# Moving the gate transposes of the second layer from one step to two and a half steps behind their silu

## The chip, the cores and the metric

The kernel runs on one core of one Trainium2 chip. The metric is the device time of one execution in microseconds, as the median of several runs: 821.22 us before (three runs, 821.09 to 822.02). Beside it stands one execution taken by the hardware profiler; all rows shown below are from that one.

## The reference

Two residual layers over 256 tokens of width 2048, in float32. The first is retention plus latent attention, gated by SiLU. The second, around which the change lies, is a Conformer convolution module:

```python
def layer_conformer_conv(x, norm_g, w_in, conv_w, conv_b, ln_g, ln_b, w_out):
    h = rms_norm(x, norm_g)
    a, b, gate = jnp.split(h @ w_in, 3, axis=-1)
    u = a * jax.nn.sigmoid(b)
    u = lax.conv_general_dilated(u, ...31 taps, causal, depthwise...) + conv_b
    u = jax.nn.silu(layer_norm(u, ln_g, ln_b))
    return x + (u * jax.nn.silu(gate)) @ w_out
```

Each of `a`, `b` and `gate` has 2048 columns, so `w_in` is 2048 x 6144 and `w_out` 2048 x 2048.

## The kernel before

**Products in three matmuls.** A float32 product is made from halves: `whi` is the weight rounded to the fast matmul type and `wlo` the rest; the activations are split in the same way. `mm3` (lines 193 to 195) issues three matmuls: high by high, high by low and low by high. ScalarE makes `whi` (line 167), VectorE or GpSimd makes `wlo` (`tt`, line 88). SyncE's queue loads the raw weights, 1 MB at a time, into three buffers (line 152).

**Steps and a clock.** The order on TensorE, ScalarE and VectorE is the order in which the program issues its instructions. The program keeps a clock of its own: each half of a weight unit (`half`) advances it to the next whole step, first queueing the `wlo` three steps ahead and the `whi` four steps ahead; `tick(True)` in the middle of a step advances it by a half. `later(n, f)` puts `f` on a list, and the tick at which n steps have gone by runs it, so that its instructions land in the queues at that point. A step of the second layer holds 12 matmuls with 512 columns each.

**A chunk.** `chunk` computes 512 columns for both halves of the tokens into two PSUM tiles of the pool `mm` (four tiles), in eight steps. The second layer runs eight chunks for `a` and `b` (`glu`), four for `gate`, and then the output product: its first half (`u_co1`) into the four tiles of the pool `aux`, sixteen steps, its second half in two more chunks.

**The gates.** After each of the four gate chunks, `gate(c, ps)` lets ScalarE make silu of the two PSUM tiles into two tiles of a pool of six (line 1137), scaled by the norm's factor per token. The result has tokens on the partitions; the output product wants features there. So `turned` issues eight transposes on TensorE (line 1142), which write back into the same PSUM tiles, and `place` lets ScalarE copy these into the gate buffer `cgt` (line 1147) and sets `gates[0]`, the count of gate pairs at hand.

**The convolution and its norm.** While the chunks run, VectorE computes the 31 taps of 16 channel blocks, paced by the clock. When the last sums are made (`sums_end`), `norm_conv` is put 4.5 steps ahead (`LN_LAG`). It issues two pairs of matmuls that sum over the partitions (lines 1013 and 1014), a chain on VectorE and ScalarE (`rs_chain`), and a table load for silu (line 1021). A gate chunk that ends between `sums_end` and `norm_conv` is held: its silu is issued in `norm_conv`, behind that table load. Here this is the third chunk (c = 2), whose silu is issued one and a half steps into the fourth chunk. The fourth gate (c = 3) is issued at the first step of the output product.

**What reads the gates.** From `norm_conv` on, eight pairs of channel blocks go through five stages, half a step apart, a new pair every two steps: normalize on VectorE (`za`), silu on ScalarE (`zs`, line 1035), times the gate on VectorE (`zb`, line 1040), round on ScalarE (`zr`, line 1044), subtract on VectorE (`zc`). `z_run` puts `zb` of pair j off by half a step while `gates[0]` is not above j. Pairs 0 to 3 read the gates of c = 0 and 1; pairs 4 and 5 those of c = 2; pairs 6 and 7 those of c = 3. `zrhs` gives the output product its activations and forces stages that are still open.

Of the kernel before, what the change touches and what calls it, by code (L numbers as in the profile page):

```python
# [48 lines left out]
def body(ctx, tc, a):  # L49
# [22 lines left out]
    def tmp(dt=F32):  # L72
        return tpool.tile([P, 512], dt, tag="t", name=nm("t"))
# [28 lines left out]
    def later(n, fn):  # L102
        due.append((clock[0] + n, len(due), fn))
# [1030 lines left out]
    def gate(c, ps):  # L1134
        g = [tmp(), tmp()]
        for t in range(2):
            act(g[t][:, :], ps[t][:, :], AF.Silu, scale=R1[:, t:t + 1])

        def turned():
            for i in range(4):  # L1140
                for t in range(2):
                    nc.tensor.transpose(ps[i // 2][:, (i % 2) * T + t * P:(i % 2) * T + (t + 1) * P], g[t][:, i * P:(i + 1) * P], ident[:, :])  # L1142

        def place():
            for b in range(2):
                o = (c % 2) * 1024 + b * 512
                act(cgt[c // 2][:, o:o + 512], ps[b][:, :], AF.Copy)
            gates[0] = 2 * c + 2

        later(1, turned)  # L1150
        later(1.5, place)

    for c in range(4):
        ps = chunk(u_cg[4 * c:4 * c + 4], yrhs)

        def gate_when(c=c, ps=ps):
            if held and not ln_done[0]:
                held[0].append(lambda: gate(c, ps))
            else:
                gate(c, ps)  # L1160

        later(0.5, gate_when)
# [135 lines left out]
```

## Time and profile before

| | us |
|---|---|
| median of three runs | 821.22 |
| profiled execution | 824.06 |
| its span, first to last instruction | 822.2 |
| TensorE busy | 811.8 |
| VectorE busy | 595.3 |
| ScalarE busy | 433.6 |
| GpSimd busy | 221.8 |

The profiled execution's time is 1.86 us longer than its span, which runs from the first to the last instruction. Rows of the timeline give the start, the duration, the engine (PE is TensorE, PEld its weight loads, DVE VectorE, ACT ScalarE, POOL GpSimd), the line of the kernel, the operation with its tiles and the number of instructions merged; what stands in brackets is idle time ahead of it, and what ended it. Matmuls are pipelined, and their ends are modelled, so their starts are the safer reading. The four gate sets lie in the trace at 658.7, 681.9, 711.6 and 732.5 us (line 1142); the output product begins at 729.6 us.

### The profile page before, as it was taken

To read this page: it belongs to the slowest core of one execution; us is meant where nothing else is said; L and a number is where in the kernel's file an instruction comes from. 1 tells how busy PE (TensorE), PEld (TensorE's weight loads), DVE (VectorE), ACT (ScalarE), POOL (GpSimd) and SP (SyncE) were. 2 spreads that over 40 slices of the span, in tenths; PEclk is the share of its full clock that TensorE was granted. 3 is DMA by queue.
4 is the path that set the end of the run, shared out by engine and by line. 5 is a ranking of instruction groups with operands and counts; after the bars stand their busy time and mean duration, and the time that the engine had idled before them with its cause. 6 is when DMAs were issued, how large, how long until landed. Compare 5 with 4: busy or idle time off the path is not lost.

```text
span 822.2 us, 12383 instructions
## 1 busy us (share of the span) xinstructions
PE 811.8 (99%) x4766; PEld 721.9 (88%) x4766; DVE 595.3 (72%) x1093; ACT 433.6 (53%) x621; POOL 221.8 (27%) x127
## 2 busy tenths in 40 slices
PE   8999999999999999999999999999999999899998
PEld 8999999999999999998888888888888878788886
DVE  5788565689678755575555439999999989678542
ACT  6765544537445554664545645554545554676331
POOL 0000000000000000000000188899999989200000
PEclk9999999999999999999999999999999999999999
DMA  8875445525444443456554445545554545445650
GB/s 279 294 286 176 161 159 201 198 96 211 156 154 154 155 154 136 172 206 219 191 205 166 192 176 184 204 159 201 205 188 171 196 171 196 154 164 194 246 189 26
DMA packets 24106, 150.93 MB, mean 184 GB/s; under 512 B 2800, under 2 KB 3952, under 8 KB 6896
## 3 DMA queue, kind: packets, MB, share of 16 engines
q1 hardware_dynamic: 23616, 148.03, 50.3%
q0 software_dynamic: 288, 2.10, 0.6%
q8 instruction: 37, 0.61, 0.3%
q14 instruction: 21, 0.17, 0.1%
q10 hardware_dynamic: 144, 0.03, 0.0%
HBM read 148.04 MB, written 2.10 MB: 183 GB/s over the span
## 4 chain that ended last, share of the span: by engine, by line
PE 94%; DVE 3%; ACT 2%; DMA 1%; issue 0%; SPq 0%; DVEq 0%; ACTq 0%
PE mm L195 28%; PE mm L193 28%; PE mm L194 28%; PE aux L195 2%; PE aux L193 2%; PE aux L194 2%; DVE wlo L88 1%; DMA raw<-in_w_first 1%; DVE s L88 0%; PE mm L1142 0%; DVE t L88 0%; ACT whi L167 0%; PE mm L1108 0%; PE aux L853 0%; PE aux L661 0%
## 5 line engine op out<-in xcount | busy, mean ns | idle before, releaser
L167 ACT ACTIVATE whi<-raw 128x1024 fp32r<-128x1024 f32 (+2 forms) x278 | 286.2, 1037 | 277.9 <-PE mm L195 183.2
L88 DVE TENSOR_TENSOR wlo<-raw,whi 128x1024 fp32r<-128x1024 f32 (+2 forms) x194 | 228.2, 1185 | 109.3 <-PE mm L194 52.1
L193 PE MATMUL mm<-whi,s 128*128 128x512 f32 (+1 forms) x760 | 285.8, 376 | 0.0
L195 PE MATMUL mm<-whi,s 128*128 128x512 f32 (+1 forms) x760 | 283.8, 373 | 0.0
L194 PE MATMUL mm<-wlo,s 128*128 128x512 f32 (+1 forms) x760 | 283.6, 373 | 0.0
L88 POOL TENSOR_TENSOR wlo<-raw,whi 128x1024 fp32r<-128x1024 f32 x84 | 201.5, 2412 | 34.7 <-PE mm L194 20.6
L91 DVE SCALAR_TENSOR_TENSOR aux<-s,cb,aux 128x256 f32<-128x256 f32 x480 | 190.0, 485 | 13.7 <-ACT aux L904 13.7
L193 PE MATMUL mm<-s,whi 128*128 128x256 f32 x636 | 183.4, 288 | 1.0 <-ACT whi L167 1.0
L195 PE MATMUL mm<-s,wlo 128*128 128x256 f32 x636 | 180.5, 284 | 1.3 <-DVE wlo L88 1.3
L194 PE MATMUL mm<-s,whi 128*128 128x256 f32 x636 | 179.8, 283 | 0.0
L195 PEld LDWEIGHTS mm<-whi,s 128*128 128x128 f32 x760 | 142.9, 188 | 25.2
L194 PEld LDWEIGHTS mm<-wlo,s 128*128 128x128 f32 x760 | 143.2, 188 | 23.9
L193 PEld LDWEIGHTS mm<-whi,s 128*128 128x128 f32 x760 | 143.3, 189 | 23.8
L195 PEld LDWEIGHTS mm<-s,wlo 128*128 128x128 f32 x636 | 121.7, 191 | 2.2 <-DVE wlo L88 2.2
L193 PEld LDWEIGHTS mm<-s,whi 128*128 128x128 f32 x636 | 121.8, 192 | 2.0 <-ACT whi L167 1.4
L194 PEld LDWEIGHTS mm<-s,whi 128*128 128x128 f32 x636 | 121.9, 192 | 0.6
L711 POOL MEMSET s<- 64x256 f32 x8 | 2.9, 362 | 234.2 <-PE mm L195 162.7
L890 POOL MEMSET s<- 128x30 f32 x16 | 1.1, 121 | 116.8 <-PE mm L194 101.0
L791 POOL DMA_DIRECT2D s<-in_xt x2 | 1.2, 618 | 97.2 <-PE aux L728 96.8
L193 PE MATMUL aux<-whi,s 128*128 128x512 f32 x64 | 25.0, 390 | 0.0
L195 PE MATMUL aux<-whi,s 128*128 128x512 f32 x64 | 24.9, 389 | 0.0
L194 PE MATMUL aux<-wlo,s 128*128 128x512 f32 x64 | 24.9, 389 | 0.0
(186 smaller groups left out, 550.1 us busy)
## 6 DMA issues: line engine op xcount, KB each, us to landing
raw<-in_c_in SPq DMA_DIRECT2D x48, 1024.0 KB, 4.8
raw<-in_w_in SPq DMA_DIRECT2D x36, 1024.0 KB, 4.8
raw<-in_w_out SPq DMA_DIRECT2D x16, 1024.0 KB, 4.8
raw<-in_c_out SPq DMA_DIRECT2D x16, 1024.0 KB, 4.8
raw<-in_w_rv SPq DMA_DIRECT2D x8, 1088.0 KB, 4.9
raw<-in_w_kvb SPq DMA_DIRECT2D x4, 1024.0 KB, 4.8
raw<-in_w_first SPq DMA_DIRECT2D x7, 512.0 KB, 4.9
raw<-in_w_qb SPq DMA_DIRECT2D x3, 1024.0 KB, 4.9
```

Of the source, the lines that this page charges most:

```text
L88: (eng or V).tensor_tensor(out=out, in0=in0, in1=in1, op=op)
L91: V.scalar_tensor_tensor(out=out, in0=in0, scalar=s, in1=in1, op0=op0, op1=op1)
L167: act(hi[:, :], self.raw[u][:, h * n:(h + 1) * n], AF.Copy)
L193: mm(ps, lh, rh, start=start, stop=False, skip_group_check=True)
L194: mm(ps, lh, rl, start=False, stop=False, skip_group_check=True)
L195: mm(ps, ll, rh, start=False, stop=stop, skip_group_check=True)
L711: G.memset(krz(i)[64 * b:64 * b + 64, :], 0.0)
L791: G.dma_start(x1[i][:, :], a["xt"][:, i * 2048:(i + 1) * 2048])
L890: G.memset(upad(c, 0, TAPS - 1), 0.0)
```

## The change

The two delays of `gate` grow. `later` counts from the tick that issued the silu: the transposes go from 1 to 2.5 steps behind it, and the evacuation with the count of gates from 1.5 to 3 steps. Nothing else is edited.

```diff
@@ -1147,8 +1147,8 @@
                 act(cgt[c // 2][:, o:o + 512], ps[b][:, :], AF.Copy)
             gates[0] = 2 * c + 2
 
-        later(1, turned)
-        later(1.5, place)
+        later(2.5, turned)
+        later(3, place)
 
     for c in range(4):
         ps = chunk(u_cg[4 * c:4 * c + 4], yrhs)
```

## The prediction

> **What bounds the kernel now.** I read the page first, then TensorE's waits, then the timeline around each of the four sets of gate transposes, and last the queues of ScalarE and VectorE behind them.
>
> ```profile
> span 822.2 us, 12383 instructions
> PE   811.8 (99%) x4766; PEld 721.9 (88%) x4766; DVE 595.3 (72%) x1093; ACT 433.6 (53%) x621; POOL 221.8 (27%) x127
> PE 94%; DVE 3%; ACT 2%; DMA 1%; issue 0%; SPq 0%; DVEq 0%; ACTq 0%
> PE mm L1142 <- ACT t L1137: 3.1, 5, 1.9
> PE mm L195 <- DVE wlo L88: 1.3, 3, 0.8
> ```
>
> (Span, busy time by engine and the chain of waits by engine are from the page; the last two rows are TensorE's waits: microseconds in all, times, longest.) TensorE holds 94% of the chain, so the time is its instruction stream plus its pauses. The largest pause in its waits is the one that the diff touches: the transposes (line 1142) wait for the silu (line 1137). A listed wait is only the idle part; the loss is read from starts, against a set that does not wait. That is the second set (c = 1), TensorE's rows in the timeline (start, duration):
>
> ```profile
> 655.13 0.39 PE L195 MATMUL mm<-whi,s 128*128 128x512 f32 x1
> 657.85 0.39 PE L195 MATMUL mm<-whi,s 128*128 128x512 f32 x1
> ...
> 681.69 0.39 PE L195 MATMUL mm<-whi,s 128*128 128x512 f32 x1
> 681.92 1.03 PE L1142 MATMUL mm<-ident,t 128*128 128x128 f32 x8
> 682.72 0.48 PE L193 MATMUL mm<-whi,s 128*128 128x512 f32 x1
> ```
>
> The first two rows are the last matmuls of two successive steps: 12 matmuls in 2.72 us, a pitch of 0.227. One step of the program's clock is such a group. From 681.69 to 682.72 are 1.03 us: one pitch and 0.80 for eight transposes. That price stays wherever they stand.
>
> **The change part by part.** It removes and adds no instruction. Four sets of 8 transposes move in TensorE's queue from 1 to 2.5 steps behind their silu, past 18 matmuls (4.08 us), and four pairs of evacuations (line 1147) from 1.5 to 3 steps in ScalarE's. No DMA is issued by either; nothing is moved past one of SyncE's or GpSimd's instructions.
>
> Sets 0, 2 and 3, TensorE, then ScalarE's rows that they wait for:
>
> ```profile
> 658.73 0.33 PE L1142 MATMUL mm<-ident,t 128*128 128x128 f32 x1 [0.48 <-ACT t L1137]
> 660.04 0.48 PE L193 MATMUL mm<-whi,s 128*128 128x512 f32 x1
> 662.65 0.39 PE L195 MATMUL mm<-whi,s 128*128 128x512 f32 x1
> ...
> 709.35 0.39 PE L195 MATMUL mm<-whi,s 128*128 128x512 f32 x1
> 711.63 0.33 PE L1142 MATMUL mm<-ident,t 128*128 128x128 f32 x1 [1.89 <-ACT t L1137]
> 712.21 0.98 PE L1142 MATMUL mm<-ident,t 128*128 128x128 f32 x7 [0.25 <-ACT t L1137]
> 712.95 0.48 PE L193 MATMUL mm<-whi,s 128*128 128x512 f32 x1
> 717.14 0.39 PE L195 MATMUL mm<-whi,s 128*128 128x512 f32 x1
> ...
> 732.13 0.39 PE L195 MATMUL aux<-whi,s 128*128 128x512 f32 x1
> 733.82 0.48 PE L193 MATMUL aux<-whi,s 128*128 128x512 f32 x1
> ```
> ```profile
> 656.69 1.28 ACT L1137 ACT_TABLE_LOAD   x1
> 657.99 1.27 ACT L1137 ACTIVATE t<-mm,R 128x512 f32<-128x512 f32 x2
> ...
> 709.60 1.28 ACT L1021 ACT_TABLE_LOAD   x1
> 710.89 1.27 ACT L1137 ACTIVATE t<-mm,R 128x512 f32<-128x512 f32 x2
> 712.05 1.06 ACT L167 ACTIVATE whi<-raw 128x1024 fp32r<-128x1024 f32 x1
> ...
> 716.52 1.07 ACT L1147 ACTIVATE s<-mm 128x512 f32<-128x512 f32 x2
> ...
> 731.78 1.24 ACT L1137 ACTIVATE t<-mm,R 128x512 f32<-128x512 f32 x2
> ```
>
> (The fourth set's transposes wait too; its 732.13 row is the last matmul ahead of them.)
>
> 1. Set 0: from 657.85 to 660.04 are 2.19; less 1.03, **1.16 us** lost. ScalarE had a table load and two silus to do, to 659.26. In the new place (2.5 steps after the step's start at 655.36) the transposes come up at 662.16: 2.9 us after the silus. The loss goes.
> 2. Set 2: 712.95 less 709.35 is 3.60; less 1.03, **2.57 us**. This silu waits behind the convolution's norm (its factor's chain, a table load), to 712.16. TensorE would pass 709.58 without a pause and have 18 matmuls more, to 713.66: 1.5 us after the silus. It goes.
> 3. Set 3: 733.82 less 732.13 is 1.69; less 1.03, **0.66 us**. Silus end at 733.02; new place 732.36 plus 4.08, 736.44. It goes. Set 1 loses nothing now and nothing then.
> 4. The clock behind set 2. From the first to the twelfth matmul, set 0 took 662.65 less 660.04, 2.61 us; set 2 took 717.14 less 712.95, 4.19. The difference is **1.58 us**, and the stretches (TensorE, weight loads, VectorE, ScalarE, GpSimd busy; then granted clock) name it:
>
> ```profile
> 682.72:701.76 19.04, 19.04 (x87) 15.78 (x86) 17.51 (x37) 9.78 (x12) 16.69 (x8) 1.00 0.54 194
> 709.58:712.95 3.37, 1.23 (x9) 0.88 (x9) 3.23 (x6) 3.34 (x4) 0.00 (x0) 1.00 0.04 15
> 712.95:717.14 4.19, 4.19 (x14) 3.28 (x13) 3.14 (x5) 2.72 (x6) 0.00 (x0) 0.59 0.64 203
> 732.36:733.82 1.46, 1.22 (x10) 0.88 (x9) 1.46 (x3) 1.46 (x3) 0.00 (x0) 1.00 0.81 213
> 733.82:760.00 26.18, 26.18 (x118) 21.67 (x117) 21.36 (x26) 17.21 (x25) 0.00 (x0) 1.00 0.52 189
> ```
>
> The clock was 0.59 right behind the only long pause, and 1.00 behind the sets with short ones or none. I take it that the pause causes it, and count it in full; its bounds are 0 and 1.58.
>
> [...]
>
> 5. Where the stall goes: weights. TensorE now runs 4.15 us further ahead of VectorE, which splits the weights (wlo) behind the same norm chain:
>
> ```profile
> 704.73 1.62 DVE L88 TENSOR_TENSOR wlo<-raw,whi 128x1024 fp32r<-128x1024 f32 x1 [4.50 <-PE mm L194]
> 712.20 1.22 DVE L88 TENSOR_TENSOR wlo<-raw,whi 128x1024 fp32r<-128x1024 f32 x1
> 715.12 1.23 DVE L88 TENSOR_TENSOR wlo<-raw,whi 128x1024 fp32r<-128x1024 f32 x1 [0.32 <-PE mm L194]
> 722.82 0.68 DVE L88 TENSOR_TENSOR s<-s,t 128x512 f32<-128x512 f32 x1
> 726.47 0.69 DVE L88 TENSOR_TENSOR s<-s,s 128x512 f32<-128x512 f32 x1 [0.50 <-ACT s L1035]
> 728.22 0.69 DVE L88 TENSOR_TENSOR s<-s,t 128x512 f32<-128x512 f32 x1
> raw<-in_c_out SPq DMA_DIRECT2D x16, 1024.0 KB, 4.8
> ```
>
> A split is queued three steps ahead of its matmuls. The one at 712.20 ends at 713.42 and serves the step that starts one step after the new transposes: 713.66 and 0.80 and 2.72, 717.2. Margin 3.8 us. From there VectorE needs 5.40 per two steps (722.82 to 728.22), of which 0.50 is a wait on ScalarE, against TensorE's 5.44; lagging, it can lose that wait and catch up. So the margin holds at 3 to 4 us. ScalarE's whi at 712.05 is queued four steps ahead, with a step more of room. A raw tile asked for when the 712.20 split frees its buffer lands 4.8 us later, at 718.2; its first reader, a whi, is queued one step after 717.2, at 719.9, and has four steps to do its work. Cost 0.
>
> 6. The evacuations: ScalarE spends the same time on them; a pair falls 1.5 steps later and behind a weight copy that waits for the very step in which the transposes run, so it adds no wait there. What reads them (line 1040) asks for set 3's part 3.5 steps later, 9.5 us, and for set 2's 6 steps later. The silu tiles are held 4.1 us longer; the next request of that pool after set 2 is set 3's, 6.5 steps on. Behind sets 0 and 1 one tile of squares per pair of channel blocks is asked for, and six buffers hold that beside two silu tiles. PSUM's pair is wanted by another chunk no sooner than five steps after the new evacuation. Cost 0; without this cover, a pair's 1.07 us (716.52) once.
>
> Sum: 1.16 + 2.57 + 0.66 + 1.58 = 5.97. The profiled execution took 824.06 for a span of 822.2; it would take 818.1. The median of the plain runs, 821.22, lies 2.84 below the profiled execution; with the same difference, **815.3 us**.
>
> **The rivals.**
>
> A. The half clock is not in plain runs, or not from the pause. The 2.84 between profiled and plain runs has room for it; against it, no other stretch shows a clock like it. Gain 4.39: 816.8. [...]
>
> B. The wait moves to the weights in part: the split behind the norm is later for TensorE than I count by over 3.8 us. Then the gain of set 2 is mostly lost; sets 0 and 3 stay with 1.82 and perhaps 1 more: about 818.5. Against it: in TensorE's whole wait list, wlo costs 1.3 us.
>
> C. It does not do what it says: the silus of set 2 end after 713.66 too, since the 1.5 us of margin is the smallest. Then only 4.08 of the delay is covered, so hardly anything is left to lose; only if the silus follow TensorE (something later in its queue holds ScalarE) would nothing change: 821.2. The norm chain starts from matmuls that stay in front, which speaks against it.
>
> D. Slower: VectorE sets the pace from the norm to the last layer's product. TensorE gives back the 4.15 us in pieces at wlo, and each piece brings a stretch at 0.59 like the one above, 1.58 each. With four, 5.97 less 4.15 less 6.32 is a loss of 4.5: 825.7; with two, 822.6. It decides from the point where VectorE's two steps cost over 5.44. For it: 5.40 now. Against it: its 0.50 of waiting, and GpSimd's 0.00 in that stretch, so nothing slows VectorE there.
>
> **How the numbers follow.** Forecast 0.64 (815.3; from 814.3, as the plain runs differ by 0.9 among themselves, to 816.2), A 0.22, B 0.07, C 0.04, D 0.03. From 814.3 to 817.8 holds the forecast and A and some of B. A measurement here tells about 0.2%, 1.64 us, from no change: faster means under 819.6. The forecast, A and nearly all of B are faster: 0.92. C and a little of B and D (two stretches) are the same: 0.05; D's rest is slower: 0.03.
>
> **What would show it.** Right: the transposes' wait on the silu gone from TensorE's list; 1.03 us from the matmul ahead of each set to the one behind it; granted clock 1.00 throughout the stretch after the norm; the last matmul some 6 us earlier. Step 4 is wrong if a slow stretch stays without a pause. Step 5 is wrong if waits on wlo or whi appear between the norm and the output product. The prediction is wrong on the whole if TensorE's pauses are gone and the time is not.

## The result and the profile after

The changed kernel took 816.51 us, the median of four executions (816.11 to 816.84), against 821.62 for the kernel before (the three executions known already and a fourth of 823.09). The ratio is 0.9934, 95% interval 0.9921 to 0.9947: faster by 0.7%, or 4.4 to 6.5 us. A second set of executions of both kernels gave 0.9930 (0.9918 to 0.9943). The forecast was 815.3 us, in a range from 814.3 to 817.8.

The page of the changed kernel (span, busy time, chain of waits by engine), and TensorE's waits (microseconds in all, times, longest):

```profile
span 814.3 us, 12383 instructions
PE 808.1 (99%) x4766; PEld 720.7 (89%) x4766; DVE 594.8 (73%) x1093; ACT 434.4 (53%) x621; POOL 221.8 (27%) x127
PE 95%; DVE 2%; DMA 1%; ACT 1%; issue 0%; SPq 0%; DVEq 0%; ACTq 0%
```
```profile
PE aux L243 <- POOL ones L236: 1.0, 1, 1.0
PE mm L193 <- ACT whi L167: 0.8, 1, 0.8
PE mm L195 <- DVE wlo L88: 0.6, 2, 0.3
```

The wait of the transposes on the silu is gone from the list, and nothing has come in its place: the three rows above lie ahead of 640 us, and behind it no wait is listed. The three sets that lost time before, in TensorE's timeline:

```profile
660.02 0.39 PE L195 MATMUL mm<-whi,s 128*128 128x512 f32 x1
660.25 1.03 PE L1142 MATMUL mm<-ident,t 128*128 128x128 f32 x8
661.04 0.48 PE L193 MATMUL mm<-whi,s 128*128 128x512 f32 x1
...
710.35 0.39 PE L195 MATMUL mm<-whi,s 128*128 128x512 f32 x1
710.58 1.03 PE L1142 MATMUL mm<-ident,t 128*128 128x128 f32 x8
711.37 0.48 PE L193 MATMUL mm<-whi,s 128*128 128x512 f32 x1
...
728.94 0.39 PE L195 MATMUL aux<-whi,s 128*128 128x512 f32 x1
729.17 1.03 PE L1142 MATMUL mm<-ident,t 128*128 128x128 f32 x8
729.96 0.48 PE L193 MATMUL aux<-whi,s 128*128 128x512 f32 x1
```

From the matmul ahead of a set to the one behind it are now 1.02 us in all three: eight transposes without a wait. Behind the norm the granted clock is 1.00 throughout (the stretch's columns as in the prediction, the clock third from the end):

```profile
709.58:725.00 15.42, 15.42 (x74) 12.85 (x73) 14.61 (x19) 13.25 (x21) 0.00 (x0) 1.00 0.58 204
```

Two profiled executions differ at their start as well. The chain of waits in order of time shows it; of before, then of after, the last transposes of the second layer's first eight chunks (line 1108) and the last matmul:

```profile
640.10 0.44 PE mm L1108 x4
...
818.19 0.24 PE mm L195
```
```profile
638.19 0.44 PE mm L1108 x4
...
810.25 0.24 PE mm L195
```

At line 1108, ahead of everything that was changed, the profiled execution of before is already 1.91 us late; why stays open. From there to the last matmul it takes 178.09 us and the changed one 172.06: **6.03 us** less. I call this the tail below, and use it for single traces, since the start drops out of it.

### The profile page after: what moved, and what is told of

It reads as the page before. It is cut to its first block, busy times and chain, and to the rows that moved or that the text cites. A ratio compares the mean times of both kernels' runs of the same rounds, so it can differ in the third digit from the quotient of the medians.

```text
span 814.3 us, 12383 instructions
## 1 busy us (share of the span) xinstructions
PE 808.1 (99%) x4766; PEld 720.7 (89%) x4766; DVE 594.8 (73%) x1093; ACT 434.4 (53%) x621; POOL 221.8 (27%) x127
## 4 chain that ended last, share of the span: by engine, by line
PE 95%; DVE 2%; DMA 1%; ACT 1%; issue 0%; SPq 0%; DVEq 0%; ACTq 0%
PE mm L195 28%; PE mm L193 28%; PE mm L194 28%; PE aux L194 2%; PE aux L193 2%; PE aux L195 2%; DMA raw<-in_w_first 1%; DVE wlo L88 1%; DVE s L88 0%; PE mm L1108 0%; PE aux L853 0%; PE mm L1142 0%; PE aux L661 0%; PE aux L759 0%; PE aux L727 0%; PE aux L728 0%
```

## The experiments

**The plain times fall into two groups.** Each execution has a mean granted clock. Beside the kernels below, the kernel before ran 72 times. In 41 of these executions the clock is 0.998 or less, and their median is 822.6 us; in the other 31 it is 0.999 or 1.00, and the median is 820.9. (The groups overlap: the first begins at 821.55, the second ends at 822.28. On the four chips that were used the first group has 11 of 23, 7 of 17, 15 of 21 and 8 of 11.) Of the changed kernel there are ten executions, all at 0.999 or 1.00, with a median of 816.2.

What the mean hides is a stretch at half clock. In the profiled execution of before it is this one (length, TensorE busy, clock, DMA, GB/s):

```profile
713.44:716.84 3.40, 3.40 (x9) 0.50 0.70 214
```

In it matmuls start 0.425 us apart (five from 713.98 to 715.68) instead of 0.227. It costs 3.40 x (1 - 0.227 / 0.425) = 1.58 us when all of it lies on matmuls, and takes 1.70 / 820, or 0.2%, off the mean: so I take 0.998 as the mark of an execution with one such fall. The mean doesn't say where the fall lies, and 3 of the 57 executions of the eight kernels below without a pause over 0.78 us behind the norm are at 0.998 too. That the falls of the kernel before lie behind the third set, in somewhat over half of its executions, is read from the trace and from experiments 3 and 7, not from each execution.

Tails below are set against 177.93 us, that of the profiled execution of before, which has the half clock in it (start of the last row of line 195 in the timeline less 640.10; the changed kernel's by the same reading is 171.89).

| kernel | median us | executions at 0.998 or less | tail against before, us |
|---|---|---|---|
| before | 820.9 / 822.6 by clock | 41 of 72 | 0 |
| changed | 816.51, then 816.10 | 0 of 10 | -6.04 |
| third set alone moved | 818.95 | 0 of 5 | -3.87 |
| the others alone moved | 820.26 | 7 of 12 | -2.05 |
| pause filled with matmuls | 820.87 | 0 of 11 | -1.63 |
| 1.5 steps | 818.09 | 0 of 5 | -4.83 |
| 2 steps | 816.49 | 1 of 6 | -6.03 |
| 4 steps | 816.64 | 1 of 4 | -6.03 |
| changed, VectorE +5 additions | 816.62 | 0 of 5 | -6.03 |
| changed, VectorE +10 additions | 821.69 | 11 of 12 | -1.19 |
| third set at half a step | 823.79 | 5 of 5 | +1.22 |
| third set split | 822.41 | 9 of 11 | -0.23 |
| changed, 40 more transposes | 821.13 | 1 of 11 | -1.67 |

**1. The third set alone.** The edit to the kernel before:

```diff
-        later(1, turned)
-        later(1.5, place)
+        later(2.5 if c == 2 else 1, turned)
+        later(3 if c == 2 else 1.5, place)
```

> Only the third set (c = 2), the one held for the norm, moves to 2.5 and 3 steps. Theory: the losses belong to single sets and add up; this one carries 2.57 us of pause and 1.58 us of half clock, so the time falls by 4.15 us, and the granted clock is 1.00 behind the norm; sets 0 and 3 still wait, 1.16 and 0.66 us. Rival A (half clock not in plain runs, or of another cause): 2.57 us.

The tail fell by 3.87 instead of 4.15, and the clock stayed up in all five executions. The 0.28 that lack are at the fourth set, which now waits longer than it did:

```profile
728.02 0.33 PE L1142 MATMUL mm<-ident,t 128*128 128x128 f32 x1 [0.31 <-ACT t L1137]
728.60 0.98 PE L1142 MATMUL mm<-ident,t 128*128 128x128 f32 x7 [0.25 <-ACT t L1137]
```

Before, that set's first transpose had no idle time listed:

```profile
732.51 0.33 PE L1142 MATMUL mm<-ident,t 128*128 128x128 f32 x1
733.08 0.98 PE L1142 MATMUL mm<-ident,t 128*128 128x128 f32 x7 [0.24 <-ACT t L1137]
```

TensorE now comes to it sooner, while ScalarE's silu still stands behind work that VectorE does late. In ScalarE's rows of the same trace:

```profile
726.30 1.09 ACT L1035 ACTIVATE s<-s,cb 128x256 f32<-128x256 f32 x2 [0.20 <-DVE s L88]
727.30 1.24 ACT L1137 ACTIVATE t<-mm,R 128x512 f32<-128x512 f32 x2
```

So the losses are not quite independent: part of a pause removed at one set comes back at the next, unless that one has the room too, as it has in the full change. The plain median, 818.95, is 1.9 below the 820.9 of the full-clock group, where 2.57 less 0.28 were due. Its five executions lie between 818.07 and 820.32, so they don't settle the tenths.

**2. The other sets alone.**

```diff
-        later(1, turned)
-        later(1.5, place)
+        later(1 if c == 2 else 2.5, turned)
+        later(1.5 if c == 2 else 3, place)
```

> Sets 0, 1 and 3 move, the third set stays one step behind its silu. Theory: the time falls by 1.16 + 0.66 = 1.82 us; the pause of the third set and the stretch at 0.59 behind it are as before, since the norm's chain starts from TensorE's own matmuls and moves with them. Rival: the norm's chain hangs on VectorE's sums and does not move; then the 1.16 us of set 0 come back as a longer pause at the third set, and only 0.66 us are gained.

The tail fell by 2.05, near the 1.82 of the theory and far from the rival's 0.66. The third set's pause is the same to a few hundredths (1.89 and 0.22 against 1.89 and 0.25), so the norm's chain did move with TensorE. From the timeline, and the stretch at half clock:

```profile
709.01 0.36 PE L1142 MATMUL mm<-ident,t 128*128 128x128 f32 x1 [1.89 <-ACT t L1137]
```
```profile
709.18:712.58 3.40, 3.18 (x12) 0.50 0.24 48
```

The half clock stays as well, in 7 of 12 executions: 820.75 us is the median of these, 819.36 that of the rest. In this trace it began sooner, partly while TensorE still waited (3.18 us busy of the 3.40), and cost less: from the matmul ahead of the set to the twelfth behind it are 7.61 us (706.74 to 714.35), and 7.79 before (709.35 to 717.14). That is 0.18 of the 0.23 by which the tail beats the theory.

**3. The pause filled.**

```diff
         def turned():
+            if c == 2:
+                d = auxps()
+                for _ in range(9):
+                    nc.tensor.matmul(d[:, :], yh[0][:, 0:P], yh[0][:, 512:1024], start=True, stop=True)
             for i in range(4):
```

> The kernel before, with nine matmuls of 512 columns into an unused bank (nothing reads them) ahead of the third set's transposes, 9 x 0.227 = 2.04 us: TensorE is busy while it would wait, and the transposes start no earlier. Theory (the pause lowers the clock): no stretch below 1.00 behind the norm, time down by 1.58 us with the pause's 2.57 us still lost. Rival (the clock falls for another reason, or not in plain runs): no change of the time, or up by what the nine matmuls exceed the pause.

The theory held. The transposes come as late as before, 71.52 us behind line 1108 against 71.53, but the clock stays at 1.00 in the trace, and at 0.999 or 1.00 in the mean of all eleven executions:

```profile
707.77 2.20 PE L1143 MATMUL aux<-s 128*128 128x512 f32 x9
709.82 0.33 PE L1146 MATMUL mm<-ident,t 128*128 128x128 f32 x1
710.39 0.98 PE L1146 MATMUL mm<-ident,t 128*128 128x128 f32 x7 [0.25 <-ACT t L1137]
```
```profile
708.00:716.00 8.00, 7.75 (x38) 1.00 0.35 134
```

The tail is 1.63 shorter, by 1.58 due. The plain median of 820.87 is that of the kernel before in its full-clock executions, 820.9. So here it was the pause that lowered the clock: it fell in 41 of 72 executions with the pause and in 0 of 11 with it filled, and with it that part of the loss went, and only that part.

**4. One and a half steps.**

```diff
-        later(1, turned)
-        later(1.5, place)
+        later(1.5, turned)
+        later(2, place)
```

> All four sets at 1.5 steps, the evacuation at 2. Theory: half a step more, 1.36 us, covers sets 0 and 3 in full (1.16 and 0.66) and leaves 2.57 - 1.36 = 1.21 us of pause at the third set. If that shorter pause leaves the clock at 1.00, the time falls by 1.16 + 0.66 + 1.36 + 1.58 = 4.76 us; if the clock still falls, by 3.18 us.

```profile
709.30 0.33 PE L1142 MATMUL mm<-ident,t 128*128 128x128 f32 x1 [0.53 <-ACT t L1137]
709.88 0.98 PE L1142 MATMUL mm<-ident,t 128*128 128x128 f32 x7 [0.25 <-ACT t L1137]
```
```profile
708.00:716.00 8.00, 7.22 (x36) 1.00 0.34 132
```

The pause is 0.78 us and the clock stays. The tail is 4.83 shorter, by 4.76 due.

**5. Two steps and four steps.** The same two lines with 2 and 2.5, and with 4 and 4.5.

> All four sets at 2 steps, the evacuation at 2.5. Theory: the third set comes up 1 x 2.72 us later than before, 712.30 us in the trace of before against silus that end at 712.16: 0.14 us of margin, so the pause is gone just so, the clock stays at 1.00 in all executions, and the time is that of the changed kernel, 816.5 us. Rival (the releasing signal needs more than 0.14 us): some tenths of a us more, with a small wait in TensorE's list.

> All four sets at 4 steps, the evacuation at 4.5. Theory: once the silus are done ahead of the transposes, more delay neither gains nor costs, until a reader of the gates comes up: the nearest are the gate products of the fourth set, which come 3.5 steps behind its evacuation at 3 steps and so 2 steps behind it at 4.5. 816.5 us, no wait on the silu. Rival (silu tiles or PSUM held longer are missed): a new wait, and over 817 us.

Both are level with the changed kernel: tails 6.03 shorter, 816.49 and 816.64 us. With two steps the margin is as small as it was counted. ScalarE's silus, then TensorE's transposes:

```profile
708.07 1.27 ACT L1137 ACTIVATE t<-mm,R 128x512 f32<-128x512 f32 x2
```
```profile
709.49 1.03 PE L1142 MATMUL mm<-ident,t 128*128 128x128 f32 x8
```

The silus end at 709.34, 0.15 us ahead, and the transposes run without idle time. With four steps nothing that holds the silu tiles, the PSUM pair or the gate buffer longer was missed. Between two and four steps the delay did not matter. In each of the two kernels one execution had a clock of 0.998 and took some 1.4 us more; its trace was not kept, so why stays open.

**6. Room in VectorE's queue.** The changed kernel with additions that do nothing useful behind the norm's chain, five in one run and ten in another:

```diff
         for f in held[0]:
             f()
+        for _ in range(5):
+            tt(sv, x1[0][:, 0:512], x1[1][:, 0:512], ALU.add)
```

> The changed kernel with five idle additions of 128 x 512 on VectorE (into a buffer that nothing reads any more) behind the norm's chain, 0.60 us each by the pitch of such rows: 3.0 us of delay ahead of the weight splits. Theory (margin of the split 3.8 us): no wait of TensorE on wlo there, 816.5 us. Rival D (VectorE is near the pace): the 3.0 us come out in TensorE's waits, 819.5 us or more.

> As the run with five, with ten additions: 6.0 us. Theory: 6.0 - 3.8 = 2.2 us of wait on wlo one step behind the third set's transposes, 818.7 us, and where that pause lowers the clock, 1.6 us more. Rival (VectorE catches up at once, or the splits have more room than I read): no change from 816.5 us.

The additions were longer than expected, some 0.71 us from one to the next and not 0.60. VectorE's rows with five, then with ten:

```profile
708.20 3.59 DVE L88 TENSOR_TENSOR e<-s,s 128x512 f32<-128x512 f32 x5
711.71 0.69 DVE L88 TENSOR_TENSOR s<-s,t 128x512 f32<-128x512 f32 x1
```
```profile
708.48 7.22 DVE L88 TENSOR_TENSOR e<-s,s 128x512 f32<-128x512 f32 x10
715.62 0.68 DVE L88 TENSOR_TENSOR s<-s,t 128x512 f32<-128x512 f32 x1
716.34 0.69 DVE L88 TENSOR_TENSOR s<-s,e 128x512 f32<-128x512 f32 x1
716.95 1.22 DVE L88 TENSOR_TENSOR wlo<-raw,whi 128x1024 fp32r<-128x1024 f32 x1
...
719.93 0.68 DVE L88 TENSOR_TENSOR s<-s,t 128x512 f32<-128x512 f32 x1
...
724.74 0.68 DVE L88 TENSOR_TENSOR s<-s,t 128x512 f32<-128x512 f32 x1
```

So the delays are 3.51 and 7.14 us. In the changed kernel itself the split in question, and the first matmul that reads it:

```profile
709.12 1.22 DVE L88 TENSOR_TENSOR wlo<-raw,whi 128x1024 fp32r<-128x1024 f32 x1
```
```profile
714.43 0.39 PE L194 MATMUL mm<-wlo,s 128*128 128x512 f32 x1
```

It ends at 710.34, 4.09 us ahead. With 3.51 us of delay the time stays at 816.62. With 7.14 a wait of 7.14 less 4.09, 3.05 us, is due. TensorE, with ten additions:

```profile
714.90 0.39 PE L193 MATMUL mm<-whi,s 128*128 128x512 f32 x1
718.22 0.50 PE L194 MATMUL mm<-wlo,s 128*128 128x512 f32 x1 [2.93 <-DVE wlo L88]
```

3.32 from start to start, less a pitch of 0.23, are 3.09. It brings the half clock in 11 of 12 executions: 821.69 us, all of the gain gone. In the trace:

```profile
718.64:722.04 3.40, 3.40 (x10) 0.50 0.81 287
```

VectorE did not set the pace afterwards, though: behind its delay two steps of its work took 4.81 us (719.93 to 724.74), against TensorE's 5.44. In the changed kernel without additions it is the same, 4.80 us (712.79 to 717.59).

**7. A longer pause.** The kernel before, with the third set at 0.5 and 1 step:

```diff
-        later(1, turned)
-        later(1.5, place)
+        later(0.5 if c == 2 else 1, turned)
+        later(1 if c == 2 else 1.5, place)
```

> The kernel before with the third set at 0.5 steps instead of 1: TensorE comes to it 1.36 us sooner and waits 3.25 + 0.25 us instead of 1.89 + 0.25. [...]

```profile
710.76 0.33 PE L1142 MATMUL mm<-ident,t 128*128 128x128 f32 x1 [3.27 <-ACT t L1137]
711.33 1.76 PE L1142 MATMUL mm<-ident,t 128*128 128x128 f32 x7 [0.25 <-ACT t L1137]
```

```profile
711.04:714.44 3.40, 3.15 (x12) 0.50 0.23 48
```

I expected the longer pause to lower the clock in most executions, with 823.8 us or more where it falls. With 3.52 us of idle time it fell in five of five, 823.79 us. Together: 0.78 us of idle time, 0 of 5; 2.14, 41 of 72; 2.93, 11 of 12; 3.52, 5 of 5. (The last two ran on one chip, on which the kernel before fell in 7 of 17.)

**8. Do transposes count as idle?** At the third set of the kernel before, TensorE goes 3.37 us without an ordinary matmul (709.58 to 712.95), of which 2.14 are idle and the rest transposes. These two runs ask which of the two lengths counts. First that set, split: two transposes at 1 step, six at 2.5.

```diff
-        def turned():
-            for i in range(4):
+        def turned(part=range(4)):
+            for i in part:
...
-        later(1, turned)
-        later(1.5, place)
+        if c == 2:
+            later(1, lambda: turned(range(1)))
+            later(2.5, lambda: turned(range(1, 4)))
+            later(3, place)
+        else:
+            later(1, turned)
+            later(1.5, place)
```

> The kernel before, but of the third set only the first two transposes stay at 1 step, and the other six and the evacuation go to 2.5 and 3: the same pause of 1.89 + 0.25 us, with 0.2 us of transposes behind it instead of 0.8. If transposes count as idle for the clock gate, the stretch without an ordinary matmul shrinks from 3.37 to some 2.8 us, and the clock falls in clearly fewer executions than in the kernel before (18 of 40 with 0.998 or less). If they count as busy, it falls as often: about half, with 822.4 us where it falls and 820.8 where not.

Then the changed kernel with 40 more transposes:

```diff
         def turned():
+            if c == 2:
+                d = auxps()
+                for n in range(40):
+                    nc.tensor.transpose(d[:, n % 4 * P:(n % 4 + 1) * P], g[n % 2][:, 0:P], ident[:, :])
             for i in range(4):
```

> The changed kernel with 40 more transposes (into an unused bank, nothing reads them) ahead of the third set's eight: 48 in a row, some 5.2 us without an ordinary matmul and without a pause. If transposes count as idle for the clock gate, the clock falls in every execution (0.998 or less) and the time is 816.5 + 40 x 0.109 + 1.6 = 822.5 us or more. If they count as busy, the clock stays at 1.00 and the time is 820.9 us.

With the split set the clock fell as often as ever, in 9 of 11 executions, with 822.42 us (2 of 11 with 821.35); the kernel before beside it, 15 of 21. Its stretch at half clock:

```profile
710.60:714.00 3.40, 3.26 (x9) 0.50 0.20 27
```

And 48 transposes in a row left the clock where it was, in the trace and, by the mean, in 10 of 11 executions:

```profile
711.16 4.53 PE L1143 MATMUL aux<-ident,t 128*128 128x128 f32 x40
715.52 1.04 PE L1146 MATMUL mm<-ident,t 128*128 128x128 f32 x8
716.32 0.48 PE L193 MATMUL mm<-whi,s 128*128 128x512 f32 x1
```
```profile
712.00:720.00 8.00, 8.00 (x58) 1.00 0.62 229
```

From 711.16 to 716.32 are 5.16 us without an ordinary matmul, at 1.00, and the tail is 4.37 longer than the changed kernel's, by 40 x 0.109 = 4.36 due. For the clock these transposes counted as busy.

**9. The changed kernel again.**

> The changed kernel once more, unedited, for more executions beside the kernel before on one chip. Theory: no pause behind the norm, so the clock stays at 0.999 or 1.00 in nearly all executions (with 2 and with 4 steps one execution in ten had 0.998 and some 1.4 us more); 816.5 us. Against the kernel before that is 4.4 us less where its clock stays (820.9) and 6.0 less where it falls (822.6).

816.10 us, six executions from 815.36 to 817.19, none below 0.999.

## Why the prediction was right, and where it was off

**The pauses (parts 1 to 3)** were right: 1.16, 2.57 and 0.66, 4.39 in all. The sets pass in 1.02 us, the tail is 6.03 shorter where 5.97 were counted, and experiments 1, 2 and 4 take the sum apart, to 0.3 us. What the parts did not say is that they hang together: with the third set alone moved, the fourth waits 0.3 us longer.

**The margins** were right: 1.5 us between the silus and the third set (709.08, from the silus' row below, to 710.58), 0.14 with two steps, measured 0.15.

```profile
707.81 1.27 ACT L1137 ACTIVATE t<-mm,R 128x512 f32<-128x512 f32 x2
```

**The clock (part 4)** was right in its cause and size, and wrong in how often. Filling the pause took 1.63 us off the tail by itself, so the pause is the cause. But with the pause of 2.14 us the clock fell in 41 of 72 executions, not in all. The step that failed is the last one, "with the same difference": the profiled execution of before had the half clock, and the median of the three plain runs, 821.22, looks like that of a full-clock execution (group median 820.9; none of the 41 is under 821.55; the clocks of these three runs are not on record). I took 1.58 us off a time that did not hold it. Taking off 4.39 alone gives 816.8, which is rival A; 816.51 was measured. Against the group with the half clock, 822.6, the whole 5.97 give 816.6. Both ways lead to the changed kernel's time, and by the forecast's way one reads 1.2 us too little: 816.51 lies above the 814.3 to 816.2 that the forecast claimed for itself, and inside the range because that took in rival A. A's number came nearer by the luck of which three executions gave the median; neither of its reasons held, since the half clock is in plain runs and comes from the pause. Of the 2.84 between the profiled execution and the plain median 1.58 were the clock; the other 1.26 fit the late start (line 1108 comes at 640.10, and at 638.7 in the median of the fourteen traces).

**Why the clock falls (also part 4).** Part 4 took the pause as the cause, and that held: with the idle 2.14 us the clock fell in 41 of 72 executions, with the pause filled in 0 of 11. The stretch of 3.37 us without an ordinary matmul was a coincidence; the idle 2.14 in it are what counts, since 5.16 us of transposes kept the clock at 1.00 (experiment 8). What part 4 did not count is the chance: a pause of 2.14 or 2.93 us lowered the clock in a part of the executions, one of 3.52 in five of five. By what rule the clock falls was not shown.

**The weights (part 5)** were right: no wait on wlo behind the norm, and a margin of 4.09 us where 3.8 were counted (the split is read by the second matmul of its step, and the step begins somewhat later). The margin lies between the delays of five and of ten additions, 3.51 and 7.14, and the ten showed what rival B would have cost. Rival D was mis-sized: its "5.40 now" is a pace that TensorE set, not VectorE's. When VectorE is late it needs 4.81 per two steps, since its 0.50 of waiting goes and more runs back to back; so it catches up, and no repeated waits came even behind a delay of 7.14 us.

**The evacuations (part 6)** were right: up to four steps later cost nothing.

## What to carry to other kernels

In a queue that runs in order, work that only feeds a later stage belongs at least the producer's own latency behind it, that of the worst place included: here every delay from 2 to 4 steps was worth the same, while less cost the pause and, with one step, in 41 of 72 executions a stretch at half clock. Before a sum is set against a median, it should be asked whether the profiled execution and the median hold the same events; a mean clock of 0.998 against 1.00 was 1.7 us here. And how near another engine is to setting the pace can't be read from its period while it waits for the first one; the durations back to back tell it (VectorE's two steps: 5.40 us with its waiting, 4.81 without).

## What the runs showed of the hardware

Behind the norm TensorE's granted clock fell to 0.50 after idle time of 2.14 us and more, but not in every execution, and in more of them where the pause was longer (0 of 5 at 0.78 us, 41 of 72 at 2.14, 11 of 12 at 2.93, 5 of 5 at 3.52). In all five traces that show a fall behind the norm it lasted 3.40 us, and it began between 2.1 us (third set split, 708.47 to 710.60) and 3.9 us (before, 709.58 to 713.44) after the pause begins, so in some it fell when TensorE was busy again. It cost up to 1.58 us by the starts of the matmuls (0.425 us apart for 0.227), and this is most of the 1.7 between the two groups of plain times of the kernel before. Transposes of 128 x 128 in float32 kept the clock up as matmuls did (5.16 us of them at 1.00 in the trace, and 10 of 11 executions at 0.999 or 1.00).

Ten additions on VectorE that write the same 128 x 512 buffer came 0.71 us apart, where most rows of that shape are followed by the next in 0.60 (721.26 to 721.86 in the trace with ten additions). Two rows of the kernel's own that write one tile in turn, the second reading it too, are 0.72 apart as well (715.62 and 716.34 with ten additions); that the shared buffer is the reason was not tried.
